# Nineteen order edges in a hybrid SSD and attention layer: small loads, state loads, attention halves, scan steps

## The chip, the cores and the metric

One core of a Trainium2 chip runs the whole program. The metric is the device time of one execution in microseconds. A run of the kernel here is three executions with their median; the profile is of one further execution. Engines are named as the profile names them: PE is TensorE, DVE is VectorE, ACT is ScalarE, POOL is GpSimd, SP is SyncE, which issues most transfers; ACT issues transfers too.

## What is computed

One layer for a prompt of 512 positions and 64 sample positions (8 sequences of 8 steps), 576 columns in all, width 1024:

```python
h = x + 0.5 * swiglu(rmsnorm(x, ffn1_norm), ...)
z, xbc, dt_raw, q, k, v, f_raw, g_ssd, g_att = split(rmsnorm(h, mix_norm) @ w_in)
xc   = silu(conv_b + sum(xa[:, j:j + L] * conv_w[j] for j in range(4)))   # xa: old rows, then xbc
y_ssd = rms_per_group((scan(xc) + d_skip * x) * silu(z)) * ssd_norm       # 4 groups, chunks of 128
y_att = fox_attention(q, k_all, v_all, logf_all)                          # 2048 cached rows for samples
h = h + (sigmoid(g_ssd) * (y_ssd @ w_ssd_proj) + sigmoid(g_att) * (y_att @ w_attn_proj)) @ w_out
y = h + 0.5 * swiglu(rmsnorm(h, ffn2_norm), ...)
```

It also returns the new keys, values, gates, SSD states and the last convolution rows.

## The kernel before

Activations lie with features on the 128 partitions and the 576 columns along the row, in two halves of 288 (`hs(0)`, `hs(1)`). Each float32 product is three matmuls of 128x288 (`mm3`, L212 to L214): high times high, low times high, high times low. A high part is a rounded copy, made by ACT; a low part is the remainder, made by DVE or, for a share of the weights, by POOL (`whi` L177, `wlo` L178; `xh` L224; `yh` L1210 and `yl` L1211 for the attention output; `ygh` L1283 and `ygl` L1284 for the gated scan output). Eight tiles of weights make 24 matmuls for a half.

The stages in order of time: the start (inputs turned on PE and scaled, small constants loaded), the first feed forward layer with the turning of the old SSD states beside it (`turns`, L365 to L389), the projections, the attention, the six convolution tiles of group 0, the attention projection, then four rounds of a group's scan with the next group's convolution tiles and output product, then the output projection and the second feed forward layer.

A convolution tile (`conv_tile`, L1135) is what most of the change hangs on. PE makes two halves into accumulators that share two banks. DVE scales the first half out of its bank (L1149) and the second in two pieces (L1154, L1156). PE turns the last columns (L1162) into the rest of the second half's bank, ACT copies that out (`tt`, L1164), and only then is that bank free. ACT starts the convolution (`kf`, L1173), DVE adds three more taps (L1175), ACT takes the tanh (L1176), and DVE makes the result in two pieces (L1177, L1179). The six tiles of a group are listed in `convs` in the order of B, C and four x tiles, so `convs[1]` is the C tile and `convs[2]` the first x tile of group 0. They write `bT`, `cT` and `xg`.

A group's scan (`group_scan`) takes the sample chunk c = 4 first, then chunks 0 to 3. A chunk makes C.B (L1307), turns x (L1330), makes its weights `dk` (L1319 to L1321) and `xdt` (L1333), multiplies (L1346, L1348) and carries the state (L1359). `state` gives the sample outputs (L1373), copied to `oo` (L1383) and turned (L1393). `gate` sums squares on POOL (L1273, L1274), `halves` makes `ygh` and `ygl`, and `group_out` begins with `rowscale`, whose matmuls L261 and L263 read these sums.

Nothing here is issued in the order of the text. A scheduler in the framework puts every engine's instructions in an order by priorities; `soon()` raises the priority, and `behind(later, first)` adds an edge that only says that `later` is put behind `first` in that order, with no wait of its own on the chip. In the kernel before all eight attention halves (`c` a copy on POOL, `h` the `yh` on ACT, and the `yl` on DVE) hang behind one tile:

```python
for x, first in zip((c, h, V.tensor_tensor(lo, y, hi.bitcast(F32), ALU.subtract)), convs[2]):
    behind(x, first)
convs.append((first, tanh, last))
```

## Time and profile before

| | us |
|---|---|
| median of 3 runs | 1869.49 (1869.19 to 1870.69) |
| the profiled execution, its own time | 1870.09 |
| its span in the trace | 1868.2 |
| PE busy | 1824.8 (98% of the span) |
| DVE busy | 1064.6 (57%) |
| ACT busy | 742.1 (40%) |
| POOL busy | 605.7 (32%) |

In the profile, times count from the start of the span. A row of the timeline gives start, duration, engine, line, operation, the tile written and the tiles read, a shape, how many such instructions follow each other, and in brackets how long the engine stood idle before it and what ended that. Engine names with a q (ACTq, SPq) are the issuing of transfers. PEclk is the clock that PE was granted, as a share of full speed. Starts of neighbouring 128x288 matmuls are some 0.13 us apart at full speed and 0.24 at half of it. The matmuls' ends are modelled and overlap.

### The profile page before, as it was taken

What the parts mean: (1) busy time and instruction counts of PE and PEld (TensorE: products, weight loads), DVE (VectorE), ACT (ScalarE), POOL (GpSimd) and SP (SyncE); (2) the same over time, 40 slices, a digit from 0 to 9 for tenths busy, and PEclk for the clock granted to TensorE, in tenths of its full rate; (3) what the DMA queues carried; (4) which work ended last, traced back from release to release, by engine and by line L of the source; (5) the groups of instructions that cost most, each with busy time, mean ns of one, the idle gap of its engine ahead of it and who ended that gap; (6) DMA issues with size and microseconds to landing.
All of it is one profiled execution on the core that took longest, in us unless ns stands there. A gap on an engine that the chain in (4) does not pass through costs nothing.

```text
span 1868.2 us, 38772 instructions
## 1 busy us (share of the span) xinstructions
PE 1824.8 (98%) x15335; PEld 1725.6 (92%) x15335; DVE 1064.6 (57%) x2309; ACT 742.1 (40%) x1555; POOL 605.7 (32%) x681
## 2 busy tenths in 40 slices
PE   7999999999999999999999999989999999999998
PEld 7999999999889888888898888878989999999998
DVE  4643334443425677876737969787695454344542
ACT  4333223334323555554426645555433333123322
POOL 0433002312322334442224644746454222002210
PEclk9999999999999999999999999999999999999999
DMA  5354443345525678885356544354472434554342
GB/s 155 121 124 127 130 138 111 119 139 164 141 80 175 190 231 244 237 227 172 91 151 185 155 125 138 103 148 139 135 216 86 124 115 131 145 144 123 109 121 67
DMA packets 297722, 269.71 MB, mean 144 GB/s; under 512 B 55068, under 2 KB 262092, under 8 KB 297388
## 3 DMA queue, kind: packets, MB, share of 16 engines
q1 hardware_dynamic: 229712, 184.16, 35.3%
q10 hardware_dynamic: 57828, 46.10, 8.0%
q0 software_dynamic: 10000, 36.97, 6.4%
q8 instruction: 121, 1.98, 0.5%
q14 instruction: 61, 0.50, 0.1%
HBM read 223.72 MB, written 38.73 MB: 140 GB/s over the span
## 4 chain that ended last, share of the span: by engine, by line
PE 63%; DVE 7%; ACT 1%; DMA 1%; issue 1%; POOL 0%; ACTq 0%; SPq 0%; DVEq 0%; POOLq 0%
PE acc L212 13%; PE acc L214 12%; PE acc L213 12%; PE pv L213 4%; PE pv L214 4%; PE pv L212 4%; PE tr L955 2%; PE tr L942 2%; PE mm L878 1%; DMA ab<-cumD 1%; PE pv L909 1%; PE mm L896 1%; DVE kf L1175 1%; PE tr L982 1%; PE pv L993 1%
## 5 line engine op out<-in xcount | busy, mean ns | idle before, releaser
L177 ACT ACTIVATE whi<-stage 128x512 fp32r<-128x512 f32 (+2 forms) x474 | 294.0, 622 | 714.8 <-PE acc L213 603.7
L212 PE MATMUL acc<-xh,whi 128*128 128x288 f32 x1792 | 541.7, 302 | 7.3 <-DVE xr L1149 4.0
L213 PE MATMUL acc<-xl,whi 128*128 128x288 f32 x1792 | 534.0, 298 | 0.0
L214 PE MATMUL acc<-xh,wlo 128*128 128x288 f32 x1792 | 532.8, 297 | 0.0
L178 DVE TENSOR_TENSOR wlo<-stage,whi 128x512 fp32r<-128x512 f32 (+1 forms) x373 | 263.7, 707 | 269.8 <-ACT whi L177 249.4
L212 PEld LDWEIGHTS acc<-xh,whi 128*128 128x128 f32 x1792 | 339.1, 189 | 14.1 <-DVE xr L1149 5.1
L213 PEld LDWEIGHTS acc<-xl,whi 128*128 128x128 f32 x1792 | 339.2, 189 | 2.9 <-issue 2.7
L214 PEld LDWEIGHTS acc<-xh,wlo 128*128 128x128 f32 x1792 | 338.8, 189 | 1.1 <-issue 0.5
L178 POOL TENSOR_TENSOR wlo<-stage,whi 128x512 fp32r<-128x512 f32 (+1 forms) x101 | 137.9, 1366 | 286.0 <-ACT whi L177 280.1
L345 POOL TENSOR_TENSOR u<-u,s 128x288 f32<-128x288 f32 x88 | 81.5, 926 | 429.0 <-DVE u L344 372.9
L212 PE MATMUL pv<-xh,whi 128*128 128x288 f32 (+1 forms) x720 | 214.1, 298 | 2.3 <-ACT xh L224 2.1
L214 PE MATMUL pv<-xh,wlo 128*128 128x288 f32 (+1 forms) x720 | 213.0, 296 | 0.0
L213 PE MATMUL pv<-xl,whi 128*128 128x288 f32 (+1 forms) x720 | 213.0, 296 | 0.0
L212 PEld LDWEIGHTS pv<-xh,whi 128*128 128x128 f32 (+1 forms) x720 | 135.0, 188 | 3.0 <-ACT xh L224 2.4
L213 PEld LDWEIGHTS pv<-xl,whi 128*128 128x128 f32 (+1 forms) x720 | 134.9, 187 | 1.2
L214 PEld LDWEIGHTS pv<-xh,wlo 128*128 128x128 f32 (+1 forms) x720 | 135.1, 188 | 0.3
L212 PE MATMUL pv<-hh,whi 128*128 128x288 f32 x352 | 106.0, 301 | 0.0
L347 POOL TENSOR_TENSOR hl<-u,hh 128x288 fp32r<-128x288 f32 x88 | 79.3, 903 | 77.5 <-ACT hh L346 77.5
L213 PE MATMUL pv<-hl,whi 128*128 128x288 f32 x352 | 104.3, 296 | 0.0
L212 PE MATMUL acc<-hh,whi 128*128 128x288 f32 x352 | 104.2, 296 | 0.0
L213 PE MATMUL acc<-hl,whi 128*128 128x288 f32 x352 | 104.2, 296 | 0.0
L214 PE MATMUL acc<-hh,wlo 128*128 128x288 f32 x352 | 104.2, 296 | 0.0
(364 smaller groups left out, 3609.8 us busy)
## 6 DMA issues: line engine op xcount, KB each, us to landing
stage<-in_w_in_dram SPq DMA_DIRECT2D x52, 512.0 KB
stage<-in_ffn_w_up_dram SPq DMA_DIRECT2D x44, 512.0 KB
stage<-in_ffn_w_gate_dram SPq DMA_DIRECT2D x43, 512.0 KB
stage<-in_ffn_w_down_dram SPq DMA_DIRECT2D x40, 512.0 KB
h<-in_state_ssm_dram SPq DMA_DIRECT2D x64, 256.0 KB
hTD<-hT ACTq DMA_DIRECT2D x32, 256.0 KB
pb<-pastD SPq DMA_DIRECT2D x32, 256.0 KB
ab<-cumD SPq DMA_DIRECT2D x32, 256.0 KB
```

The costliest lines, as they stand in the source:

```text
L177: act(hi, view, AF.Copy)
L178: e.tensor_tensor(lo, view, hi.bitcast(F32), ALU.subtract)
L212: mm(out, lhsT=hi, rhs=a, start=first and i == 0, stop=False)
L213: mm(out, lhsT=hi, rhs=b, start=False, stop=False)
L214: mm(out, lhsT=lo, rhs=a, start=False, stop=last and i == n - 1)
L345: G.tensor_tensor(u, u, sil[half], ALU.mult)
L347: G.tensor_tensor(hl[:, hs(half)], u, hh[:, hs(half)].bitcast(F32), ALU.subtract)
L878: mm(s[:, :n], lhsT=q, rhs=ks[2 * self.p + e][:, :n], start=hl == 0, stop=hl == 1)
L896: nc.tensor.transpose(t[:, j * P:(j + 1) * P], lt[:, j * P:(j + 1) * P], ident)
L909: mm(self.ob[o:o + 32, i * P:(i + 1) * P], lhsT=vtok[j][:, v0:v0 + 32], rhs=self.pts[e][:, j * P:(j + 1) * P], start=j == 0, stop=j == i)
L942: nc.tensor.transpose(t[:, i * P:(i + 1) * P], kk[:, i, p * P:(p + 1) * P], ident)
L955: mm(s[kv * 32:(kv + 1) * 32, :], lhsT=self.q(kv), rhs=self.kT[kv // 2], start=True, stop=True)
```

## The change

It adds edges, moves three loads to another queue, and changes no arithmetic. In the diff `ev` is L1156, `turned` L1162, `cb` L1307, `x` L1330 and then L1393, `own` L1346, `m1` and `m2` are L261 and L263, and `lows` are the `ygl`.

- A. Three small loads on ACT (`bb` twice, `al`; L497, L498, L502) go behind the eighth `xh` of the start.
- B. The first three loads of old states (L379) are issued by ACT instead of SP.
- C. The eight attention halves (copy, `yh`, `yl`) go behind `convs[1]` to `convs[4]`, two each, instead of all behind `convs[2]`.
- D. The last two `ygl` of the first half (`lows[2:4]`) go behind L1156 of the next group's B tile.
- E. C.B and three of the x turns of the sample chunk go behind the turned columns (L1162) of the group's own x tiles.
- F. Three of the four turns of `oo` (L1393) go behind the first product of a later chunk.
- G. The matmuls of `rowscale` in groups 0 to 2 go behind L1162 of the next group's C tile.

```diff
-            q.dma_start(out=bb[:32], in_=A["dt_bias"].rearrange("o h -> h o"))
-            q.dma_start(out=bb[32:48], in_=A["b_f"].rearrange("o h -> h o"))
+            behind(q.dma_start(out=bb[:32], in_=A["dt_bias"].rearrange("o h -> h o")), nrm1.insts[7])
+            behind(q.dma_start(out=bb[32:48], in_=A["b_f"].rearrange("o h -> h o")), nrm1.insts[7])
...
-            q.dma_start(out=al[:32], in_=A["a_log"].rearrange("o h -> h o"))
+            behind(q.dma_start(out=al[:32], in_=A["a_log"].rearrange("o h -> h o")), nrm1.insts[7])
...
-                        nc.sync.dma_start(out=tiles[n], in_=ap3(A["state_ssm"][0], *place(n % 2, n // 2)))
+                        (nc.scalar if n < 3 else nc.sync).dma_start(out=tiles[n], in_=ap3(A["state_ssm"][0], *place(n % 2, n // 2)))
...
-        convs.append((first, tanh, last))
+        convs.append((first, tanh, last, ev, turned))
...
-                for x, first in zip((c, h, V.tensor_tensor(lo, y, hi.bitcast(F32), ALU.subtract)), convs[2]):
+                for x, first in zip((c, h, V.tensor_tensor(lo, y, hi.bitcast(F32), ALU.subtract)), convs[1 + n // 2]):
                     behind(x, first)
...
+                if c == 4:
+                    behind(cb, convs[6 * g + 2][4])
...
+                    if c == 4 and i < 3:
+                        behind(x, convs[6 * g + 3 + i][4])
...
+                    if r == 0:
+                        owns.append(own)
...
+                if i < 3:
+                    behind(x, owns[i + 2])
...
+            if first is not None:
+                behind(m1, first)
+                behind(m2, first)
...
-            rg = rowscale(ysq, 1.0 / 512, ysq)
+            rg = rowscale(ysq, 1.0 / 512, ysq, convs[6 * g + 7][4] if g < 3 else None)
...
+                for x in lows[2:4]:
+                    behind(x, convs[6 * g + 6][3])
```

What it makes of the order is seen at three places. Lines of the changed kernel are higher by 2 at L261, by 5 around L1149 to L1211, by 7 at L1330.

**DVE, convolution tiles of group 0.** The accumulators `acc_2231` and `acc_2232` are the halves of the third x tile, `xr_2210`, `xr_2219` and `xr_2230` the first three x tiles. Before:

```order
L1211 TENSOR_TENSOR yl_2245_12103<-qy_1293_7508,yh_2244_12102 128x576
L1211 TENSOR_TENSOR yl_2247_12108<-qy_1420_8071,yh_2246_12107 128x576
L1211 TENSOR_TENSOR yl_2249_12113<-qy_1547_8637,yh_2248_12112 128x576
L1211 TENSOR_TENSOR yl_2251_12118<-qy_1674_9203,yh_2250_12117 128x576
L1211 TENSOR_TENSOR yl_2253_12123<-qy_1801_9769,yh_2252_12122 128x576
L1149 TENSOR_TENSOR xr_2230_11948<-acc_2231_11951,rbc_901_5369 128x288
L1211 TENSOR_TENSOR yl_2255_12128<-qy_1928_10335,yh_2254_12127 128x576
L1211 TENSOR_TENSOR yl_2257_12133<-qy_2055_10901,yh_2256_12132 128x576
L1211 TENSOR_TENSOR yl_2259_12138<-qy_2156_11390,yh_2258_12137 128x576
L1175 SCALAR_TENSOR_TENSOR kf_2223_11928<-xr_2219_11865,P2_80_293,kf_2223_11928 128x600 x2
L178 TENSOR_TENSOR wlo_2264_12150<-stage_2261_12143,whi_2263_12149 128x512
L1175 SCALAR_TENSOR_TENSOR kf_2223_11928<-xr_2219_11865,P2_80_293,kf_2223_11928 128x600
```

Now, from the end of the first x tile:

```order
L1184 SCALAR_TENSOR_TENSOR xg_2203_11773<-xr_2210_11786,kf_2214_11849 128x64
L1216 TENSOR_TENSOR yl_2249_12113<-qy_1547_8637,yh_2248_12112 128x576
L1216 TENSOR_TENSOR yl_2251_12118<-qy_1674_9203,yh_2250_12117 128x576
L1180 SCALAR_TENSOR_TENSOR kf_2223_11928<-xr_2219_11865,P2_80_293,kf_2223_11928 128x600
L1154 TENSOR_TENSOR xr_2230_11948<-acc_2231_11951,rbc_901_5369 128x288
L1180 SCALAR_TENSOR_TENSOR kf_2223_11928<-xr_2219_11865,P2_80_293,kf_2223_11928 128x600 x2
L178 TENSOR_TENSOR wlo_2264_12150<-stage_2261_12143,whi_2263_12149 128x512
L1159 TENSOR_TENSOR xr_2230_11948<-acc_2232_11977,rbc_901_5369 128x224
L1161 TENSOR_TENSOR xr_2230_11948<-acc_2232_11977,rbc_901_5369 128x8x8
L1182 SCALAR_TENSOR_TENSOR xg_2203_11773<-xr_2219_11865,kf_2223_11928 128x512
L1184 SCALAR_TENSOR_TENSOR xg_2203_11773<-xr_2219_11865,kf_2223_11928 128x64
L1216 TENSOR_TENSOR yl_2253_12123<-qy_1801_9769,yh_2252_12122 128x576
```

Of the six `yl` between the first x tile and the third tap of the second, two are left there. One pair now stands behind the C tile, ahead of these rows, and two pairs behind later tiles. The L1149 of the third x tile (now L1154) stands behind two `yl` and one tap where it stood behind five `yl`.

**PE, the same place.** Here the rows carry what they wait for: a semaphore of DVE or of ACT. Before:

```order
L214 MATMUL acc_2231_11951<-xh_898_5358,wlo_2229_11945 128x288
L1162 MATMUL acc_2221_11894<-ident_2_76,xr_2219_11865 91x128 [waits DVE_49]
L1330 MATMUL mm_2351_12741<-ident_2_76,xg_2203_11773 64x128 [waits DVE_49]
L212 MATMUL acc_2232_11977<-xh_793_4687,whi_2226_11940 128x288 [waits DVE_49]
L213 MATMUL acc_2232_11977<-xl_794_4688,whi_2226_11940 128x288
...
L214 MATMUL acc_2232_11977<-xh_898_5358,wlo_2229_11945 128x288
L212 MATMUL acc_2240_12030<-xh_793_4687,whi_2235_12019 128x288 [waits Activation_49]
L213 MATMUL acc_2240_12030<-xl_794_4688,whi_2235_12019 128x288
```

Now:

```order
L214 MATMUL acc_2231_11951<-xh_898_5358,wlo_2229_11945 128x288
L1167 MATMUL acc_2221_11894<-ident_2_76,xr_2219_11865 91x128 [waits DVE_49]
L1337 MATMUL mm_2351_12741<-ident_2_76,xg_2203_11773 64x128 [waits DVE_49]
L212 MATMUL acc_2232_11977<-xh_793_4687,whi_2226_11940 128x288 [waits Activation_49]
L213 MATMUL acc_2232_11977<-xl_794_4688,whi_2226_11940 128x288
...
L214 MATMUL acc_2232_11977<-xh_898_5358,wlo_2229_11945 128x288
L212 MATMUL acc_2240_12030<-xh_793_4687,whi_2235_12019 128x288 [waits DVE_49]
L213 MATMUL acc_2240_12030<-xl_794_4688,whi_2235_12019 128x288
```

PE's order is the same. The second half of the third x tile waited for DVE, for the L1149 of its own first half; now it waits for ACT, for the copy `tt` of the tile before it. The half behind it has the two the other way round: the two banks are handed out in another turn.

**PE, the start of group 2's output product.** `acc_2955` and `acc_2956` are the halves of one of the next group's convolution tiles. Before:

```order
L1162 MATMUL acc_2944_15982<-ident_2_76,xr_2942_15953 91x128 [waits DVE_49]
L214 MATMUL acc_2955_16040<-xh_898_5358,wlo_2953_16034 128x288
L261 MATMUL tr_2988_16349<-ssq_2815_15409,cst_1_75 128x512 [waits PE_49,Pool_49]
L212 MATMUL acc_2956_16066<-xh_793_4687,whi_2950_16029 128x288 [waits DVE_49]
L213 MATMUL acc_2956_16066<-xl_794_4688,whi_2950_16029 128x288
L214 MATMUL acc_2956_16066<-xh_793_4687,wlo_2951_16030 128x288
```

Now:

```order
L1167 MATMUL acc_2944_15982<-ident_2_76,xr_2942_15953 91x128 [waits DVE_49]
L214 MATMUL acc_2955_16040<-xh_898_5358,wlo_2953_16034 128x288
L212 MATMUL acc_2956_16066<-xh_793_4687,whi_2950_16029 128x288 [waits DVE_49]
L213 MATMUL acc_2956_16066<-xl_794_4688,whi_2950_16029 128x288
L214 MATMUL acc_2956_16066<-xh_793_4687,wlo_2951_16030 128x288
L212 MATMUL acc_2956_16066<-xh_807_4780,whi_2950_16029 128x288
L263 MATMUL tr_2988_16349<-ssq_2815_15409,cst_1_75 128x512 [waits PE_49,Pool_49]
L213 MATMUL acc_2956_16066<-xl_808_4781,whi_2950_16029 128x288
```

The matmul that reads the sums of squares (L261, now L263) stands four matmuls later, and the first of these four is one that waits for DVE.

## Rows read from the trace of the kernel before

**Rows 1.** The page's first part: busy time, share of the span, instructions.

```profile
PE 1824.8 (98%) x15335; PEld 1725.6 (92%) x15335; DVE 1064.6 (57%) x2309; ACT 742.1 (40%) x1555; POOL 605.7 (32%) x681
```

**Rows 2.** Waits of PE: engine line, waited for, total us, times, longest us.

```profile
PE tr L261 <- POOL ssq L1274: 3.2, 1, 3.2
...
PE pv L212 <- ACT xh L224: 2.1, 1, 2.1
PE tr L1393 <- ACT oo L1383: 2.1, 1, 2.1
```

**Rows 3.** Stretches: length, busy PE, PEld, DVE, ACT, POOL, then PEclk, DMA.

```profile
911.95:918.90 6.95, 6.85 (x52) 6.54 (x52) 5.76 (x9) 3.18 (x6) 2.39 (x3) 1.00 0.02 4
933.30:936.80 3.50, 3.50 (x17) 3.50 (x17) 2.49 (x5) 0.78 (x2) 0.41 (x1) 0.54 0.01 3
...
1240.30:1243.70 3.40, 3.40 (x16) 3.39 (x15) 3.13 (x6) 0.51 (x1) 0.95 (x2) 0.50 0.82 260
```

**Rows 4.** Timeline of ACT and its issues at the start.

```profile
13.78 0.78 ACT L224 ACTIVATE xh<-h,P 128x576 fp32r<-128x576 f32 x1 [1.75 <-DMA stage<-in_ffn_w_gate_dram]
...
14.28 0.40 ACTq L502 DMA_DIRECT2D al<-in_a_log_dram  x1
...
34.04 4.87 ACTq L508 DMA_DIRECT2D pcol<-in_page_table_dram  x7
```

**Rows 5.** Waits of SP's queue, 110 to 125 us.

```profile
SPq L379 <- DMA pastD<-lg: 2.6, 2, 1.9
```

**Rows 6.** Timeline of SP's queue, 117 to 122 us.

```profile
120.85 1.47 SPq L379 DMA_DIRECT2D h<-in_state_ssm_dram  x3
```

**Rows 7.** Timeline of PE at the first turned state.

```profile
123.90 0.90 PE L385 MATMUL tr<-ident,h 128*128 128x128 f32 x4 [2.65 <-DMA h<-in_state_ssm_dram]
```

**Rows 8.** Timeline of PE in the convolution tiles of group 0.

```profile
924.11 0.40 PE L212 MATMUL acc<-xh,whi 128*128 128x288 f32 x1 [1.70 <-DVE xr L1149]
...
931.74 0.35 PE L1162 MATMUL acc<-ident,xr 128*91 128x128 f32 x1 [1.01 <-DVE xr L1156]
932.91 0.30 PE L1330 MATMUL mm<-ident,xg 128*64 128x128 f32 x1 [0.82 <-DVE xg L1179]
```

**Rows 9.** Timeline of DVE there.

```profile
920.25 3.44 DVE L1211 TENSOR_TENSOR yl<-qy,yh 128x576 fp32r<-128x576 f32 x5
923.61 0.45 DVE L1149 TENSOR_TENSOR xr<-acc,rbc 128x288 f32<-128x288 f32 x1
923.98 3.18 DVE L1211 TENSOR_TENSOR yl<-qy,yh 128x576 fp32r<-128x576 f32 x3
...
928.71 1.78 DVE L178 TENSOR_TENSOR wlo<-stage,whi 128x512 fp32r<-128x512 f32 x1
```

**Rows 10.** Timeline of ACT there.

```profile
918.65 4.69 ACT L1210 ACTIVATE yh<-qy 128x576 fp32r<-128x576 f32 x8
...
924.55 0.25 ACT L1164 ACTIVATE tt<-acc 91x128 f32<-91x128 f32 x1
```

**Rows 11.** Timeline of POOL there.

```profile
923.94 1.94 POOL L178 TENSOR_TENSOR wlo<-stage,whi 128x512 fp32r<-128x512 f32 x1 [2.86 <-ACT whi L177]
928.25 1.70 POOL L178 TENSOR_TENSOR wlo<-stage,whi 128x512 fp32r<-128x512 f32 x1 [2.37 <-ACT whi L177]
```

**Rows 12.** Line L1211: count, duration least, median and most in ns.

```profile
L1211 DVE TENSOR_TENSOR yl<-qy,yh x8: 744/746/1850, 920.3 to 926.4; 128x576 fp32r<-128x576 f32 x8
```

**Rows 13.** Timeline of DVE in the scan of group 1.

```profile
1129.04 3.54 DVE L1284 SCALAR_TENSOR_TENSOR ygl<-xg,P,ygh 128x288 fp32r<-128x288 f32 x4
1132.50 0.45 DVE L1149 TENSOR_TENSOR xr<-acc,rbc 128x288 f32<-128x288 f32 x1
```

**Rows 14.** Timeline of PE in the scan of group 2.

```profile
1224.32 0.45 PE L1346 MATMUL pv<-dk,xdt 128*64 128x128 f32 x4
```

**Rows 15.** Timeline of ACT there.

```profile
1220.02 1.28 ACT L1319 ACTIVATE dk<-ab,TT 128x128 f32<-128x128 f32 x4 [7.15 <-DMA ab<-cumD]
```

**Rows 16.** Timeline of DVE ahead of group 2's output product.

```profile
1238.90 0.45 DVE L1149 TENSOR_TENSOR xr<-acc,rbc 128x288 f32<-128x288 f32 x1
```

More of the change, by code (lines that the diff above doesn't have):

```diff
@@ L214, in mm3, with hilo @@
             mm(out, lhsT=lo, rhs=a, start=False, stop=last and i == n - 1)
-    def hilo(hp, view, tagh, tagl, scale=None, n=NT, bufs=None):
+    def hilo(hp, view, tagh, tagl, scale=None, n=NT, bufs=None, insts=None):
         hi = tl(hp, [P, n], F32R, tag=tagh, bufs=bufs)
@@ L223, in hilo @@
         else:
-            act(hi, view, AF.Copy, scale=scale)
+            h = act(hi, view, AF.Copy, scale=scale)
             V.scalar_tensor_tensor(lo, view, scale, hi.bitcast(F32), ALU.mult, ALU.subtract)
+            if insts is not None:
+                insts.append(h)
         return hi, lo
@@ L255, in spread, with rowscale @@
         return r
-    def rowscale(s, inv, r):
+    def rowscale(s, inv, r, first=None):
         with soon():
             t = tr()
-            mm(t, lhsT=C("one"), rhs=s[:, :NP], start=True, stop=True)
+            m1 = mm(t, lhsT=C("one"), rhs=s[:, :NP], start=True, stop=True)
             t2 = sm()
-            mm(t2[:, :NS], lhsT=C("one"), rhs=s[:, NP:], start=True, stop=True)
+            m2 = mm(t2[:, :NS], lhsT=C("one"), rhs=s[:, NP:], start=True, stop=True)
+            if first is not None:
+                behind(m1, first)
+                behind(m2, first)
             V.transpose(r[:, :NP], t)
@@ L275, in __init__ @@
         def __init__(self, wcol, sqp=None, xsp=xp):
-            self.wcol, self.xs, self.n, self.sqp, self.xsp = wcol, [], 0, sqp, xsp
+            self.wcol, self.xs, self.n, self.sqp, self.xsp, self.insts = wcol, [], 0, sqp, xsp, []
         def add(self, h, squares=True):
             k = self.n
-            self.xs.append(hilo(self.xsp, h, "xh", "xl", scale=P1[:, self.wcol + k:self.wcol + k + 1]))
+            self.xs.append(hilo(self.xsp, h, "xh", "xl", scale=P1[:, self.wcol + k:self.wcol + k + 1], insts=self.insts))
             self.n += 1
@@ L1155, in conv_tile @@
         with soon():
-            V.tensor_tensor(xsamp[:, :, 3:], a[:, NP - HT:].rearrange("p (b t) -> p b t", t=T),
+            ev = V.tensor_tensor(xsamp[:, :, 3:], a[:, NP - HT:].rearrange("p (b t) -> p b t", t=T),
                             rbc[:, NP:].rearrange("p (b t) -> p b t", t=T), ALU.mult)
@@ L1161, in conv_tile @@
             t = full[:n, 512 - P:]
-            nc.tensor.transpose(t, xr[:, NP:], ident)
+            turned = nc.tensor.transpose(t, xr[:, NP:], ident)
             tt = tl(xz, [n, P], tag="tt", bufs=1)
@@ L1262, in group_scan @@
             ysq = tl(sa, [P, NT], tag="ssq", bufs=2)
-            yhl = []
+            yhl, lows, owns = [], [], []
             def gate(o0, n):
@@ L1283, in halves @@
                     act(hi, xg[:, i, hs(half)], AF.Copy, scale=w)
-                    V.scalar_tensor_tensor(lo, xg[:, i, hs(half)], w, hi.bitcast(F32), ALU.mult, ALU.subtract)
+                    lows.append(V.scalar_tensor_tensor(lo, xg[:, i, hs(half)], w, hi.bitcast(F32), ALU.mult, ALU.subtract))
             def operands(x, bp):
@@ L1306, in chunk @@
                 s = sm()
-                mm(s[:n, :n], lhsT=bT[:, o0:o0 + n], rhs=cT[:, o0:o0 + n], start=True, stop=True)
+                cb = mm(s[:n, :n], lhsT=bT[:, o0:o0 + n], rhs=cT[:, o0:o0 + n], start=True, stop=True)
+                if c == 4:
+                    behind(cb, convs[6 * g + 2][4])
                 cbm = tl(wk, [P, P], tag="cbm", bufs=3)
@@ L1329, in chunk @@
                 for i in range(4):
-                    nc.tensor.transpose(t[:n, i * P:(i + 1) * P], xg[:, i, o0:o0 + n], ident)
+                    x = nc.tensor.transpose(t[:n, i * P:(i + 1) * P], xg[:, i, o0:o0 + n], ident)
+                    if c == 4 and i < 3:
+                        behind(x, convs[6 * g + 3 + i][4])
                 xdt = tl(wk, [P, 8, 64], tag="xdt", bufs=2)
@@ L1345, in chunk @@
                     ov = yb[(r % 2) * 64:(r % 2 + 1) * 64, (r // 2) * n:(r // 2 + 1) * n]
-                    mm(ov, lhsT=xdt[:n, r, :], rhs=dks[r // 4][:n, r % 4, :n], start=True, stop=not 0 < c < 4)
+                    own = mm(ov, lhsT=xdt[:n, r, :], rhs=dks[r // 4][:n, r % 4, :n], start=True, stop=not 0 < c < 4)
+                    if r == 0:
+                        owns.append(own)
                     if 0 < c < 4:
@@ L1392, in group_scan @@
             for i in range(4):
-                nc.tensor.transpose(t[:, i * P:(i + 1) * P], oo[:, i * P:(i + 1) * P], ident)
+                x = nc.tensor.transpose(t[:, i * P:(i + 1) * P], oo[:, i * P:(i + 1) * P], ident)
+                if i < 3:
+                    behind(x, owns[i + 2])
             for i in range(4):
@@ L1408, in group_scan @@
                                 in_=oo.rearrange("p (i n) -> p i n", n=P))
-            return ysq, yhl
+            return ysq, yhl, lows
         def group_out(g, ysq, ys_):
-            rg = rowscale(ysq, 1.0 / 512, ysq)
+            rg = rowscale(ysq, 1.0 / 512, ysq, convs[6 * g + 7][4] if g < 3 else None)
             cw = Cols(A["w_ssd_proj"][0], 0, k0=4 * g, nk=4)
@@ L1440, in build @@
             cur = nxt
-            gated = group_scan(g, *cur)
+            *gated, lows = group_scan(g, *cur)
             if g < 3:
                 nxt = group_in(g + 1)
+                for x in lows[2:4]:
+                    behind(x, convs[6 * g + 6][3])
             for _ in range((3, 0, 0, 5)[g]):
```

## The prediction

> **What bounds the kernel now.** PE is busy for 1824.8 of 1868.2 us [rows 1], so only the 43 us in which it stands idle can be won, and the slow stretches that follow some of them. I read three views in this order. First the waits of PE, to see which idle times the edges touch [rows 2]. Then the timeline of PE around each. A stall costs more than its idle time where the clock falls behind it: after the pair of 1.01 and 0.82 us [rows 8] and after the 3.17 us ahead of L261 PE was granted 0.54 and 0.50 of full speed for 3.5 and 3.4 us [rows 3], that is the 1.2 GHz level, worth 1.7 us each. The single stall of 1.70 us [rows 8] was not followed by one. Last the timelines of the engines that PE waited for. A difference under 0.2% (3.74 us) I call the same.
>
> **The sum, part by part.** The work is the same; every gain is a stall that goes.
>
> A, the three small loads. ACT was ready 1.75 us before its first `xh` [rows 4]; the wait stood on a small load's issue ahead of it, for a weight tile that `xh` doesn't read. Now `xh` is next on ACT and the wait falls on the weight's high part behind it. PE waited 2.13 us for that `xh` [rows 2]. At most PE is 1.8 us earlier. The bound from below is 0.95: PE's next work needs the second half of the inputs, for which the issue at 14.28 had waited too [rows 4]; they may have landed only then, 0.95 us before PE came to them. I take **1.2**. The loads now stand ahead of the eight page table loads, 0.65 to 0.7 us of ACT's queue each [rows 4]. The page indices and the weights behind them on ACT come up to 2 us later; PE first needs what hangs on them about 1.6 us after they would then be ready. If that cover is gone, each us beyond it is lost.
>
> B, three state loads on ACT. SP was free and its issue stood until 120.85 [rows 6], for stores of `pastD` [rows 5]. The issue on ACT waits for the same stores. It loses the queue's own delay and its longer first issue: three issues took 1.47 us, and the transfer that PE waited for until 123.90 [rows 7] landed 3.05 us after the first. I take **0.4**. From below it is -0.3, if the issues on ACT stand behind a late tanh; from above 1.2, if the stores' landing is not what held it. Behind them on ACT a high part and the first layer's own steps come 1 to 2 us later; PE needs that high part 8 us on. The stall keeps over 2 us, so its slow stretch stays too. The Trainium skill (DMA: Bandwidth & Descriptors, "Issuing engines are not separate DMA queues") says that issuing from several engines saves only the sequencer's time, since all land on the same 16 DMA engines. By that sentence this part is worth nothing and the sum 0.4 less; no run here has shown it yet.
>
> C, the attention halves, is the main term. In the kernel before ACT made all eight `yh` in one piece [rows 10] and `tt` came behind them at 924.55, so the bank of the second x tile was held; the third tile's second half was given the bank of its own first half instead, and waited for L1149, which stood on DVE behind five `yl` of 3.44 us [rows 9]. That is the 1.70 us stall. Three more `yl` and a slow `wlo` then made the next tile's L1156 and L1179 late: 1.01 and 0.82 us, with the slow stretch of 1.7 [rows 3, 8, 9]. Together 3.53 + 1.7 = 5.2 us. In the new order ACT has two `yh` at a time (1.2 us), so `tt` of each tile follows its L1162 by 0.3 us, and DVE has two `yl` per tile. Following the new order with the durations of the rows, the third tile's second half starts at 922.45 instead of 924.11, and the fourth's at 929.5 instead of 932.98, both after a wait of 0.35 for `tt`. L1149 has 3 us to spare, since the half that now waits for it comes a half later. The last pair of `yl` is read by the attention projection's own first product, some 2.4 us after it starts, and is ready at about that time: up to 0.5 there. I take 5.2 less 0.7 = **4.5**; bounds 2.5, with 2 us of waiting for the last pair, and 5.2.
>
> D, `ygl` behind L1156. In group 1 the four `ygl` (3.54 us) stand behind that L1156 already and still ahead of the L1149 for which PE waits until 1133.00 [rows 13]. They keep that place. Elsewhere a DVE step changes places with one of 0.4 to 0.9 us, in the first group's scan ahead of an `xdt` that PE reads. I take **-0.3**, bounds -1.5 and 1.8, the whole stall.
>
> E, C.B and the x turns. In the group where PE waits for C.B, it stood behind that L1162 already. **0**, bounds -0.3 and 1.1.
>
> F, the turns of `oo`. PE waits 2.11 us for `oo` in group 2 [rows 2]. The third turn now stands behind the next product, and PE runs on for 2.7 us of matmuls. But the next product, L1346, reads `dk`, and ACT stood idle 7.15 us until 1220.02 for its load [rows 15]; `dk` and `xdt` let L1346 begin at 1224.32 [rows 14], by ACT's and DVE's order, which is the same. PE comes there 2 us earlier and waits there. **0**, bounds -0.3 and 2.1.
>
> G, the sums of squares. L261 waited 3.17 us for POOL [rows 2] until 1239.34. The first of the four matmuls that now stand ahead of it reuses a bank that L1149 empties, and DVE came to that L1149 at 1238.90 and was done with it at 1239.35 [rows 16], behind a tap that waited for ACT. So PE still stops and goes on at the same time, and the slow stretch stays. **0**, bounds -0.3 and 4.9.
>
> Sum: 1.2 + 0.4 + 4.5 - 0.3 = 5.8. From the profiled 1870.09 that makes 1864.3; the median of the runs is 0.6 lower, so 1863.7.
>
> **The rivals.**
>
> R1: the scan edges do what they are for. Then the 2.11 and 3.17 us go, with 1.7 of slow clock [rows 2, 3]: 7.0 more, 1856.7. For it: PE has work of its own at both places. Against it: the next wait ends at the same time [rows 14, 16].
>
> R2: only the first stall of the tiles goes, since the rest of the tile's work on DVE is as late as before. A at its low end and 1.70 of C, less 0.3: 2.4, 1867.1. For it: DVE is busy 5.76 of 6.95 us in a tile without any `yl` [rows 3], and a pair adds 1.25 to 1.4 [rows 9, 12], so it is full.
>
> R3, slower: DVE becomes the bound of four tiles. Some of its steps take 1.1 us longer while POOL makes a `wlo`: one `yl` took 1850 against 744 ns, a `wlo` 1.78 [rows 9, 11, 12]. The 5.76 holds one such step; with a pair and two more a tile takes DVE 5.76 + 1.3 + 2.2 = 9.25 against PE's 6.95. Over four tiles 9.2 us, less the 3 that L1149 has to spare, is 6.2; three stalls of 2 us each followed by a slow stretch add 5.1; the 5.2 of before go, and 1.3 of A, B and D: 4.8 slower than before, 1874.3. It decides from about two more slow steps a tile. Against it: POOL makes one `wlo` in a tile, which can hold up one step of DVE. The Trainium skill (SBUF — State Buffer, "SBUF: two separate sides") says that a DVE instruction with two SBUF inputs and a GpSimd one that reads SBUF lock each other out for the whole instruction. The 1850 ns agree, and by that rule the change puts more such instructions of DVE beside POOL's.
>
> **How the numbers follow.** The forecast as summed 0.65, R1 0.10, R2 0.17, R3 0.08. The forecast's own range, from C at 2.5 with A at 0.95 and B at 0 to C at 5.2 with A at 1.8, B at 1.2, is 1866.3 to 1861.6. Of its 0.65 some 0.02 end within 3.74 of the old time. Faster: 0.63 + 0.10 = 0.73. Same: 0.17 + 0.02 = 0.19. Slower 0.08. The range for 8 in 10 takes in R1 and R2 with 1.5 us for the bounds of D: 1856.5 to 1868.5; R3 is left out.
>
> **What would show it.** Right: PE's first `pv` L212 near 13 us; no wait for L1149 over 0.5 us between 915 and 935 and full clock there, with `yl` in four pairs; PE still waiting for state loads, for a product in group 2's scan at its old time, and for a DVE step ahead of L261. Wrong: full clock after group 2's scan (R1), a stall in the tiles at another line (R2), or DVE without a gap from 905 to 935 and PE waiting in each tile (R3).

## The result and the profile after

The changed kernel took 1873.13 us (median of 20 runs, 1868.84 to 1879.58), the kernel before beside it 1869.36 us (20 runs): ratio 1.0023, 95% interval 1.0016 to 1.0031. By the ratio it is slower by 4.3 us (the two medians differ by 3.8); I had forecast 5.8 us faster, in a range that ends at 1868.5. The profiled execution is the slowest of the 20 (1879.58 us), so its own total says little; what follows is read place by place.

The page's first part, which answers [rows 1]:

```profile
PE 1833.4 (98%) x15335; PEld 1730.1 (92%) x15335; DVE 1061.0 (57%) x2309; ACT 742.8 (40%) x1555; POOL 602.9 (32%) x681
```

The instructions are the same in number, yet PE is busy for 8.6 us more. It stood in slow stretches for longer: between the start and the last stage it was granted half the clock for 30.6 us (from 122.8, 583.6, 1051.2, 1160.4 and 1249.2 us on), in the kernel before for 13.6 (from 124.1, 584.9, 933.1 and 1240.3). Half of that difference is 8.5 us. The waits of PE, with columns as in [rows 2]:

```profile
PE pv L1355 <- DVE xdt L1342: 5.2, 4, 2.4
PE acc L212 <- DVE xr L1154: 4.5, 3, 3.2
...
PE tr L390 <- DMA h<-in_state_ssm_dram: 4.2, 1, 4.2
...
PE mm L1312 <- DVE cT L1184: 2.0, 1, 2.0
```

The waits of [rows 2] for `ssq` and `oo` are gone, and that for `xh` is down to 0.25 us. These four have grown: in the kernel before they were 1.2 us for `xdt`, 4.0 for `xr`, 2.6 for the state load and 1.1 for `cT`. The timeline of PE gives their places (the brackets hold the idle time and what ended it):

```profile
123.90 1.09 PE L390 MATMUL tr<-ident,h 128*128 128x128 f32 x4 [4.22 <-DMA h<-in_state_ssm_dram]
...
927.13 0.40 PE L212 MATMUL acc<-xh,whi 128*128 128x288 f32 x1 [0.25 <-ACT tt L1169]
...
946.66 0.40 PE L212 MATMUL acc<-yh,whi 128*128 128x288 f32 x1 [1.48 <-DVE sq L1240]
...
1049.81 0.45 PE L1355 MATMUL pv<-dk,xdt 128*64 128x128 f32 x4 [2.36 <-DVE xdt L1342]
...
1158.73 0.33 PE L1312 MATMUL mm<-cT,bT 128*64 128x64 f32 x2 [2.04 <-DVE cT L1184]
...
1248.38 0.40 PE L212 MATMUL acc<-xh,whi 128*128 128x288 f32 x1 [3.16 <-DVE xr L1154]
```

Five readings. At the first states PE waits 4.22 us, where it waited 2.65 [rows 7]. In the four convolution tiles the stalls of 1.70, 1.01 and 0.82 us [rows 8] are gone; two of 0.25, for `tt`, are left. A stall of 1.48 us is new just behind the tiles, one of 2.36 in the scan of group 0. At 1158 PE waits 2.04 us for `cT`, ahead of C.B. And at 1248 PE waits as long as it had waited for `ssq`, now for L1154. Four stretches (columns as in [rows 3]):

```profile
119.60:124.00 4.40, 0.18 (x2) 0.13 (x2) 2.96 (x5) 2.48 (x6) 2.00 (x3) 0.86 0.90 245
...
126.00:129.40 3.40, 3.40 (x16) 3.40 (x16) 0.46 (x1) 0.00 (x0) 0.80 (x1) 0.50 0.46 154
...
583.60:593.80 10.20, 10.20 (x39) 8.70 (x39) 9.74 (x26) 3.64 (x8) 2.76 (x5) 0.50 0.60 155
...
1051.00:1058.00 7.00, 6.77 (x39) 3.96 (x40) 6.76 (x14) 4.22 (x14) 2.33 (x6) 0.52 0.44 118
```

Behind the stalls of 4.22 and 2.36 us PE was granted half the full speed (the 1.2 GHz level). At 583.6 us it was granted no more, and there is no stall: PE had work without a gap, small matmuls that read 24 partitions.

```profile
580.77 1.98 PE L702 MATMUL tr<-hr,bias 24*128 24x512 f32 x4
...
582.98 3.06 PE L815 MATMUL mm<-hr,vv 24*128 24x64 f32 x16
```

To place gains and losses I compare the start of the same matmul by its number in the two traces ("offset", after less before; behind 1040 us F's order gives some numbers to other matmuls): -1.6 us at 18 us, +1.0 at 129, +4.3 at 614, +4.6 at 920, +2.0 at 947, +1.6 at 1040, +6.8 at 1054, +9.8 at 1168, +7.3 at 1223, +9.1 at the end. The 3.3 us lost between 129 and 614 come in and behind the slow stretch at 587, which no edit touches; the last section comes back to it.

### The profile page after: what moved, and what is told of

The parts are those of the page before. It is cut to its first block, busy times and chain, and to the rows that moved or that the text cites. A ratio compares the mean times of both kernels' runs of the same rounds, so it can differ in the third digit from the quotient of the medians.

```text
span 1877.7 us, 38792 instructions
## 1 busy us (share of the span) xinstructions
PE 1833.4 (98%) x15335; PEld 1730.1 (92%) x15335; DVE 1061.0 (57%) x2309; ACT 742.8 (40%) x1555; POOL 602.9 (32%) x681
## 4 chain that ended last, share of the span: by engine, by line
PE 65%; DVE 5%; DMA 2%; ACT 1%; issue 1%; POOL 0%; ACTq 0%; SPq 0%; DVEq 0%
PE acc L212 13%; PE acc L214 13%; PE acc L213 13%; PE pv L213 4%; PE pv L214 4%; PE pv L212 4%; PE tr L960 2%; PE tr L947 2%; PE mm L883 1%; DMA ab<-cumD 1%; PE pv L914 1%; PE mm L901 1%; PE pv L1355 1%; DVE kf L1180 1%; PE tr L987 1%; PE pv L998 1%
## 5 line engine op out<-in xcount | busy, mean ns | idle before, releaser
L212 PE MATMUL acc<-xh,whi 128*128 128x288 f32 x1792 | 542.0, 302 | 7.3 <-DVE xr L1154 4.5
L212 PEld LDWEIGHTS acc<-xh,whi 128*128 128x128 f32 x1792 | 339.7, 190 | 14.2 <-DVE xr L1154 6.4
L212 PE MATMUL pv<-xh,whi 128*128 128x288 f32 (+1 forms) x720 | 214.0, 298 | 0.2 <-ACT xh L224 0.2
L212 PEld LDWEIGHTS pv<-xh,whi 128*128 128x128 f32 (+1 forms) x720 | 134.9, 187 | 0.9 <-ACT xh L224 0.5
L212 PE MATMUL pv<-hh,whi 128*128 128x288 f32 x352 | 105.9, 301 | 0.0
L212 PE MATMUL acc<-hh,whi 128*128 128x288 f32 x352 | 104.1, 296 | 0.0
```

The source lines that it names most:

```text
L212: mm(out, lhsT=hi, rhs=a, start=first and i == 0, stop=False)
```

## The experiments

Each ratio below is to the kernel before, run beside it on the same chip, with its 95% interval; chips differ by up to 6 us, so times are not compared across chips. Part letters are the prediction's.

**The parts alone.** Four kernels with one part of the diff each; D to G went together.

> Only the three small loads are moved (A). The prediction's theory: 1.2 us faster than before (0.95 to 1.8), PE's first product of the first layer near 13 us, the rest of the trace as before and merely earlier. Rival: the start is earlier by 1.5 us but the wait for the old states, 2.65 us at 123.9 before, takes it back because their landing does not move with PE; then that wait is above 4 us and the time is within 0.5 us of before. Told apart by the start of the first matmul after the state load and by the length of that wait.

> Only the first three state loads are issued by ACT (B). The prediction's theory: 0.4 us faster (-0.3 to 1.2), the wait for the first state load 2.2 us. Rival, from the trace of the whole change, where that wait grew to 4.22 us while the fourth state load went out on SP at 118.65, just before the three on ACT at 118.75: the fourth load is no longer behind the first three and shares the transfer engines with them, so the first lands 5 us after its issue and not 3; the wait is 3 to 4.5 us, the stretch at half clock behind it longer, and the time 0.5 to 2.5 us more than before.

> Only the attention halves are spread over four tiles (C). The prediction's theory: 4.5 us faster (2.5 to 5.2), no wait over 0.5 us in the convolution tiles nor behind them. Rival, from the trace of the whole change: the stalls of 1.70, 1.01 and 0.82 us and the stretch at half clock go, but the last pair of low halves and the taps put with them make DVE late for the attention projection's first results, with a wait of 1.5 us at L1235 and one of 0.4 us at a low half; then 2.5 to 3.3 us faster.

> Only the edges of the scans (D to G). The prediction's theory: within 0.5 us of before, the waits of group 2 at their old places. Rival, from the trace of the whole change, where PE's lead over before shrank by some 5.5 us between 1042 and 1058 and by 2.7 us between 1140 and 1165 and grew by 0.5 later: these edges cost 4 to 8 us, with a wait of 2 us or more for xdt in the scan of group 0 followed by a stretch at half clock. If that wait is absent here and the time is as before, it belonged to that one execution or to the change's other parts, which shift when transfers land.

| kernel | ratio | interval |
|---|---|---|
| A | 0.9999 | 0.9988 to 1.0010 |
| B | 1.0019 | 1.0009 to 1.0029 |
| C | 0.9988 | 0.9976 to 1.0000 |
| D to G | 1.0018 | 1.0008 to 1.0027 |

The four differences add up to +0.0024, the whole change has +0.0023: it loses by B and by the scan's edges, and C gains less than these cost. b_alone, c_alone and scan_alone went the way of their rivals, scan_alone with 3.4 us by its ratio where its rival had 4 to 8. a_alone's time can't tell its two theories apart; its wait for the states was 2.88 us, not the over 4 of its rival. The order of instructions shows one thing more: D, E or G by itself leaves every engine's order as it was. The order of D to G together is that of F alone, which moves steps on all engines and in all four groups. The later place of `rowscale`'s matmul in group 2, which the prediction puts down to G, comes with F.

**B: which load is late.** On SP alone the first load was issued at 120.85 [rows 6] and PE had its tile 3.05 us later [rows 7]. After the change (the queues of SP and ACT in the timeline):

```profile
118.65 6.73 SPq L384 DMA_DIRECT2D h<-in_state_ssm_dram  x2
...
118.75 1.53 ACTq L384 DMA_DIRECT2D h<-in_state_ssm_dram  x3
```

ACT issues 2.1 us earlier, and PE starts at the same 123.90: landing took 5.15 us. SP, rid of three loads, issues the fourth at the same moment. The earlier issue is not the queue's doing, since the stores ahead of it went out earlier too. The last of them before, then after, in the timeline of ACT:

```profile
116.27 0.39 ACTq L562 DMA_DIRECT2D pastD<-lg  x1
...
114.75 0.38 ACTq L567 DMA_DIRECT2D pastD<-lg  x1
```

From the last store's issue to the first load's it took 3.8 to 4.6 us in the eleven executions with the loads on SP and 3.9 to 4.4 in the eight with them on ACT, on average 4.1 in both.

This kernel puts the fourth on ACT too, behind the three:

```diff
-                        (nc.scalar if n < 3 else nc.sync).dma_start(out=tiles[n], ...
+                        (nc.scalar if n < 4 else nc.sync).dma_start(out=tiles[n], ...
```

> As B alone, but the first four state loads go out on ACT instead of three, so none goes out on SP beside them. Theory 1: with three on ACT the fourth, free to start on SP at 118.7, shares the transfer engines with the first, which then lands 5.2 to 5.8 us after its issue instead of 3 to 3.9; here the first is alone at the head of one queue and lands 3 to 4 us after 118.8, PE's wait for it is 1 to 2.5 us, and the time is within 1 us of before or up to 1.5 us less. Theory 2: ACT's queue is itself slower, behind the 32 stores of small pieces that it carries just before; then the wait stays at 3.5 us or more and the time 2 to 4 us above before, as with three.

Ratio 1.0002 (0.9991 to 1.0013). Its timeline of ACT's queue and of PE:

```profile
120.69 1.52 ACTq L384 DMA_DIRECT2D h<-in_state_ssm_dram  x3
122.45 0.37 ACTq L384 DMA_DIRECT2D h<-in_state_ssm_dram  x1
...
123.73 0.63 PE L390 MATMUL tr<-ident,h 128*128 128x128 f32 x4 [1.85 <-DMA h<-in_state_ssm_dram]
```

Landing 3.04 us, wait 1.85. Over all profiled executions, from the first issue to PE's start: 3.1 to 4.5 us in eleven with all loads on SP, 5.1 to 5.8 in three with three on ACT and the fourth on SP, 3.0 to 4.4 in five with four on ACT. PE's mean wait is 2.4, 4.2 and 2.4 us. The fourth load goes out 0.1 us ahead of the first in the three, and 1.5 to 1.8 us behind it in the other sixteen. So the fourth load beside the other three is what B costs. The slow stretch behind this wait went with its length: none in the eight executions with waits of 1.57 to 2.16 us, 3.4 us in the nine with 2.17 to 3.64, 6.8 us in the two with 4.22 and 4.82.

**C: the new stall behind the tiles.** DVE's timeline after the change, at the step that PE waits for at 946.66:

```profile
946.15 0.45 DVE L1240 SCALAR_TENSOR_TENSOR sq<-kf,acc 128x288 f32<-128x288 f32 x1 [1.94 <-DMA kf<-thD]
```

The first `th` of the attention projection takes a buffer that the taps of the tiles use (tag "kf"); it was issued at 940.41, when a tap had freed it. With a buffer of its own:

```diff
-                th = tl(mixp, [P, NT], tag="kf", bufs=2)
+                th = tl(mixp, [P, NT], tag="kf", bufs=2) if j else tl(yhp, [P, NT], tag="thl", bufs=1)
```

> As C alone, but the first load for the gate of the attention projection gets a buffer of its own and can be issued early; with C alone it shares the buffer of a convolution's taps, was issued at 933.5 and landed near 938.4, and DVE waited 1.15 us for it and PE 0.70 for DVE. Theory 1: this load is what takes back a part of C; then PE's wait at L1235 (0.70 with C alone, 1.48 with the whole change) is gone, and the time is 0.7 to 1.5 us below C alone. Theory 2: DVE is simply late after the tiles, with low halves and taps ahead; then PE's wait stays at 0.5 us or more.

Ratio 0.9984 (0.9973 to 0.9995), against 0.9988 for C: the interval now leaves 1 out. The two intervals overlap, so what the buffer is worth is read from the traces. DVE's `sq` and PE's first product there:

```profile
944.00 0.45 DVE L1240 SCALAR_TENSOR_TENSOR sq<-thl,acc 128x288 f32<-128x288 f32 x1 [0.34 <-PE acc L214]
...
940.52 0.40 PE L213 MATMUL acc<-yl,whi 128*128 128x288 f32 x1 [0.37 <-DVE yl L1216]
```

DVE now waits for PE there. PE's wait for `sq` is 0.70, 1.48 and 1.63 us in the three executions with C as it is, and gone in the five with the buffer. From 920 to 947 us the offset falls by 2.5 to 3.4 us in the three executions with C as it is and by 4.2 in all five with the buffer; in the eleven without C it moves by 0 to -1.8, on average by -0.7.

**F: where the scan's edges cost.** F's edges in group 0 only, then in group 1 only:

```diff
-                if i < 3:
+                if i < 3 and g == 0:
                     behind(x, owns[i + 2])
```

> Of the edges in the scans only the turns of the sample outputs of group 0 (F in group 0). Theory 1: F alone moves work in the scans (D, E and G leave every place as it was), and in group 0 it turns PE's short wait at those turns (0 to 2.3 us at 1041) into one of 2 us or more at the next product, where xdt stands on DVE behind four low halves that wait for ACT, with a stretch at half clock behind it: 2 to 4 us between 1040 and 1054 and 1.5 to 3.5 us in the time. Theory 2: the loss between 1040 and 1054 comes from the load of the decay rows landing late, which varies by execution; then this run loses no more there than the kernels without F (0 to 2.4 us) and its time is that of before.

> Only the turns of group 1 (F in group 1). Theory 1: the wait of 1.8 us for L1149 at 1133 goes, and in its place come waits of 1.1 us at the next tile and 1.6 to 2.0 us at C.B, with a stretch at half clock: 0.6 us won by 1138, 2.5 to 3 us lost between 1140 and 1168, 1.5 to 2.5 us slower in all. Theory 2: those waits need the delay that the edges make in group 0; then they are absent here and the time is that of before.

1.0014 (1.0004 to 1.0024) and 1.0014 (1.0001 to 1.0026). In f_g0 PE waits 2.40 us for `xdt` at 1051, as at 1049.81 above. The chain behind that wait, in the timelines of SP, ACT and DVE after the change:

```profile
1038.23 0.76 SPq L1321 DMA_DIRECT2D ab<-cumD  x1
...
1044.74 0.40 ACT L1326 ACTIVATE dk<-ab,TT 128x128 f32<-128x128 f32 x1 [5.33 <-DMA ab<-cumD]
...
1047.06 2.09 DVE L1289 SCALAR_TENSOR_TENSOR ygl<-xg,P,ygh 128x288 fp32r<-128x288 f32 x4 [2.83 <-ACT ygh L1288]
1049.08 0.68 DVE L1342 TENSOR_TENSOR xdt<-mm,TT 128x512 f32<-128x512 f32 x1
```

`xdt` stands behind four `ygl`, these wait for `ygh`, and those stand on ACT behind a `dk` that waits for its load, 6.5 us after the issue. Either the order of `ygh` and `ygl` or the load could be mended. The first:

```diff
+            for u, l in zip(ups, lows):
+                behind(u, last3["exp"])
+                behind(l, last3["xdt"])
```

(`ups` and `lows` are the `ygh` and `ygl` steps, `last3` the second `dk` Exp and the `xdt` of chunk 3.)

> Part F alone (whose order of instructions is that of D to G together, 1.0018 of the kernel before), and besides, in every group, the four early ygh of the scan put behind the second dk Exp of chunk 3 on ACT, and the four early ygl behind xdt of chunk 3 on DVE. Theory queue: F costs time because the ygl that it brings ahead of xdt wait for ygh, and these for a dk that waits for its cumD load; then the xdt wait of 2.0 to 2.4 us at about 1048 falls under 0.5 us, the local offset of 1040 to 1054 falls from +3.2..5.2 to about +1, and the ratio from 1.0018 to about 1.0005. Rival load: the late cumD load itself holds TensorE, whatever stands in the queues; then a wait of about 2 us stays there, on dk instead of xdt, and the ratio stays at 1.0014 to 1.0020. Rival elsewhere: F's cost is mostly in group 1 (f_g1 alone 1.0014); then the xdt wait goes and the ratio stays above 1.0010.

Ratio 0.9996 (0.9985 to 1.0007), and no wait there is over 0.50 us. But the load landed in 4.2 us here, so this run can't tell the two theories apart. The next three turn to the load: F's new order of SP's loads in the kernel before, by one edge on SP (`scan_order_sp`), F with the two weight loads behind that load (`scan_load_first`), and the same two loads moved in the kernel before (`load_first`).

```diff
+            if g == 1:
+                behind(staged[n0 + 10], scts[2])
```

```diff
+            if g == 0:
+                for x in staged[n0 + 10:n0 + 12]:
+                    behind(x, cums[9])
```

(`staged`, `scts` and `cums` list the `stage`, `scT` and `ab` loads; the first edit is `scan_order_sp`'s.)

> The kernel before, with none of the change's edges, and on SP alone at group 0 the order that part F brings: the second scT load ahead of the first stage load, so that the cumD load of chunk 3's second half (ab) is issued right behind that stage load (some 0.5 us after it, where it was 1.0). Theory load: F's cost in group 0 is this load's landing; then it lands 6.1 to 6.5 us after its issue (3.97 in the profile of before), TensorE waits 2.0 to 2.4 us at about 1047, and the ratio is 1.0010 to 1.0018. Theory queue: the order of ygh and ygl costs it; then the landing takes 4 to 5 us, the wait is under 0.8 us and the ratio 0.9992 to 1.0006. Third: the landing varies from one execution to the next whatever the order; then it may be anything from 4.0 to 6.5 us, and the ratio is within 0.0006 of 1.

> Part F alone (its order is that of D to G together), and in group 0 the two stage loads behind the cumD load of chunk 3's second half on SP. Theory load: it then lands 4 us or less after its issue and earlier, the wait for xdt at about 1047 goes (under 0.4 us), and the ratio falls from 1.0018 to 1.0003 to 1.0010 (group 1 keeps its own part). Theory queue: ygl still stand ahead of xdt, behind ygh behind dk; if dk's load lands late for another reason the wait stays at 1.5 to 2.4 us, and the ratio at 1.0012 to 1.0020.

> The kernel before, with none of the change's edges; only the two stage loads of group 0 behind the cumD load of chunk 3's second half on SP. Waits of 0 to 2.4 us (mean 1.2 in seven profiled executions without F in group 0) stand at about 1047 in such kernels. Theory load: they are gone here, landing 4 us or less, ratio 0.9990 to 0.9998. Rival: the weights come later by as much and TensorE waits for wlo or whi instead: ratio 1.0000 to 1.0008.

| kernel | ratio | interval | issue to `dk`, us |
|---|---|---|---|
| scan_order_sp | 1.0000 | 0.9989 to 1.0012 | 4.4 |
| scan_load_first | 0.9990 | 0.9979 to 1.0002 | 3.9 |
| load_first | 1.0008 | 0.9998 to 1.0019 | 4.4 |

Over all 19 profiled executions PE's wait at that place goes with the load's landing, whichever step it is put down to: up to 4.8 us from issue to `dk` no wait is over 0.8 us but one of 1.08, at 5.4 and 5.7 us it is 1.4 and 1.7, from 6.1 us on 2.0 to 2.4. Where it is put down to `oo`, in seven executions without F in group 0, the wait is the landing less 4.0 us; where it is put down to `xdt`, in the four with F as it stands, it is the landing less 4.1. So at a late landing F's order costs no more than the order before. But F as it stands landed in 6.1 to 6.5 us in four executions of four, F with either repair in 3.7 to 4.2 in three of three, and kernels without F in group 0 took 4.0 to 4.8 in eight of twelve and 5.4 to 6.4 in four. One of those four is f_g1, whose wait can't come from its own edges, which begin later:

```profile
1051.32 0.48 PE L1400 MATMUL tr<-ident,oo 128*128 128x128 f32 x1 [2.36 <-ACT oo L1390]
```

So F costs by this load, as far as four late landings in four against four in twelve show it, and with either repair the cost is gone; scan_load_first came out below its range of 1.0003 to 1.0010. F's order of SP's loads did not bring the cost (scan_order_sp falls to the rival), but that run is no clean test: in its trace the one edge has moved steps on every engine, 36 on DVE, and `xdt` stands ahead of a `ygl` there. Moving the load in the kernel before gains nothing (load_first falls to its rival). In the four executions of F as it stands the weight load ahead of it had stood waiting too and was issued 1.4 us after `scT`, directly ahead of `ab`; in scan_order_sp 0.5 us after it. Which of these neighbours makes it late is not settled.

f_g1's ratio is not explained either. In its profiled execution the offset stands at 11.1 us at 1058 and at 9.3 at the end, so its edges in group 1 cost nothing there, and one late load in one execution doesn't make a median of twelve.

**The parts put together.** `best` is A, C, B with four loads on ACT, and the buffer of c_own; `best_halves` adds the edges of f_halves without F, `best_load` those of load_first. `after_again` is the changed kernel once more. `mended` is the whole change, A to G, with the three repairs (four loads on ACT, own buffer, load first).

> Parts A and C, B with all four first state loads on ACT, and a buffer of its own for the first th of the attention halves; D to G left off. If the parts add up as they did for the change as a whole, -1.2 us at the start, 0 to -1 at the state loads and -3 at the four convolution tiles: ratio 0.9972 to 0.9984. If A and C interact (a part ends in slack of the other), 0.9984 to 0.9995. The waits at 924 to 947 stay under 0.5 us each; the one at 124 is 1.5 to 2.2 us.

> The kernel best, with the early ygh and ygl of every group behind chunk 3's second dk Exp and xdt, without F. Theory queue: three of the four ygl stand ahead of xdt in the kernel before too, and the xdt waits of 0 to 2.4 us at about 1048 come from there; then they are gone here and the time is 0 to 2 us below best (ratio to before 0.9965 to 0.9980). Rival load: no change against best, within 0.0008.

> The kernel best (A, C, B with four loads on ACT, own buffer for the first th), and the two stage loads of group 0 behind the cumD load. Theory load: 0 to 1.5 us below best, ratio to before 0.9966 to 0.9976. Rival: no difference from best, 0.9974 within its interval of 0.0012.

> The changed kernel once more. What belongs to its order of instructions returns: the wait of 3.5 to 4.3 us for the first state load, waits of 1.5 to 2.5 us for xdt at 1050, 1.0 to 1.5 for the convolution's accumulator or sq at 947, 2.0 for C.B at 1159, 3.2 for xr at 1248. What belongs to one execution does not: half-clock stretches of 24 matmuls at 588 and 20 at 125 need not return, and their numbers may be anything from 7 to 24. Ratio 1.0016 to 1.0031 again.

> The whole change, A to G, with three repairs: the fourth state load on ACT behind the other three, a buffer of its own for the first th, and group 0's two stage loads behind the cumD load of chunk 3's second half. Theory: the change loses by B's fourth load, by th's buffer and by that cumD load, and by nothing else; then the waits at about 122 (under 2.9 us), 947 (none) and 1050 (under 0.8 us) are mended, and the ratio is that of best and of scan_load_first together, 0.9960 to 0.9978. Rival: the order of D to G also costs something in groups 1 and 2 (C.B 2.0 us at 1159, xr 3.2 us at 1248); then A, B and C gain their 0.2 to 0.26% and the scan gives some of it back: 0.9980 to 0.9995. If neither holds, 1.0000 or more.

| kernel | ratio | interval |
|---|---|---|
| best | 0.9974 | 0.9962 to 0.9987 |
| best_halves | 0.9979 | 0.9968 to 0.9990 |
| best_load | 0.9984 | 0.9972 to 0.9995 |
| after_again | 1.0013 | 0.9999 to 1.0027 |
| mended | 0.9977 | 0.9965 to 0.9988 |

The repairs turn 1.0013 to 1.0023 into 0.9977, within the theory's range, though the interval reaches into the rival's (0.9980 to 0.9995). So the three steps are the change's loss as far as these runs can tell, and what the scan's edges cost in groups 1 and 2, if anything, is within the interval. In `mended` the three places read, in the timeline of PE, and the load on SP and ACT:

```profile
122.86 0.63 PE L391 MATMUL tr<-ident,h 128*128 128x128 f32 x4 [2.06 <-DMA h<-in_state_ssm_dram]
...
939.45 0.40 PE L214 MATMUL acc<-yl,whi 128*128 128x288 f32 x1 [0.37 <-DVE yl L1217]
...
1044.39 0.45 PE L1356 MATMUL pv<-dk,xdt 128*64 128x128 f32 x4 [0.62 <-DVE xdt L1343]
...
1033.45 0.41 SPq L1322 DMA_DIRECT2D ab<-cumD  x1
...
1037.15 0.40 ACT L1327 ACTIVATE dk<-ab,TT 128x128 f32<-128x128 f32 x1 [3.48 <-DMA ab<-cumD]
```

`best` needs none of D to G and is as fast; neither edge added to it gains; best_load misses the 0.9966 to 0.9976 of its theory. `best` and `mended` both beat the kernel before and the changed one, by 4.9 and 4.3 us against the former, by their ratios. after_again brought back the waits of the order (4.82 us for the state load, 2.05 for `xdt`, 1.63 for `sq`, 3.17 for L1154), but 1.37 for C.B where 2.0 was expected. It has a slow stretch of 6.8 us at 125 again, but only 6.8 at 586 where the first profile had 10.2. Its ratio is below the 1.0016 that was expected at least.

## Why the prediction was wrong, by its own steps

The signs that I had named for being right all came: `pv` L212 at 12.63 us, no wait for L1149 in the tiles and full clock there, `yl` in four pairs, waits for state loads, for group 2's next product and for a DVE step ahead of L261. One of them looks at a place where time was lost, the state loads, but it asks for a wait and not for its length; none looks at `th` or at group 0's scan.

**A** (1.2, bounds 0.95 to 1.8): right at its place, and smaller behind it. PE's matmul at 14.61 starts 1.2 to 2.3 us earlier in the seven executions with A (mean 1.8) and 0.5 earlier on average in those without: 1.3, of which 0.8 is left at 18 us, below my lower bound. It is too small for the run times to show.

**B** (+0.4): wrong sign, and the failed step is "It loses the queue's own delay and its longer first issue". There was no such delay to lose: between the last store and the first load lie 4.1 us on either queue, and the first issue took 0.37 us on SP and 0.41 on ACT. And I followed the three loads that moved and not the fourth that stayed. It had been issued behind them; freed of them it starts with them and the landing grows from 3.05 to 5.15 us, past my lower bound of -0.3. The slow stretch behind grows as well where the wait passes 4 us. From 117 to 129 us the three kernels with three loads on ACT lose 0.7 to 3.7 us, mean 2.4; the eleven with all loads on SP gain 1.0 on average, the five with four on ACT 0.9. The 3.4 between the first two is near B's 0.19%, which is 3.5 us, though b_alone's own profile is the 0.7. The Trainium skill (DMA: Bandwidth & Descriptors, "Issuing engines are not separate DMA queues"), which I quoted against any gain, says that loads of different engines interleave on the same 16 DMA engines. The landing times agree; taken further, that sentence warns of just this loss.

**C** (4.5): the mechanism was right. All three stalls go, `tt` leaves 0.25 to 0.36, and the last pair of `yl` costs 0.37 where I allowed 0.5. The size was off twice. The step "Together 3.53 + 1.7" took the slow stretch behind the tiles as certain; it stands there in five of eleven executions without C, behind stalls that are the same to 0.03 us in ten of them. And "the attention projection's own first product" was followed for `yl` only, not for `th`, whose load waits for a tap's buffer: 0.70 to 1.63 us. By the offsets of 920 and 947 us, with the 0.7 of the executions without C taken off, C is worth 2.1 us as it is (mean 2.8) and 3.5 with the buffer.

**D, E, G** (-0.3, 0, 0): right that they bring nothing. They move nothing, and D's forecast change of places doesn't come about. What I foresaw for G comes with F: the wait for `ssq` became one of 3.16 us for L1154, as said with [rows 16].

**F** (0): right in group 2, where I looked. PE runs on and waits at the next product, for `xdt`, where it had waited 2.11 us for `oo`:

```profile
1233.29 0.45 PE L1355 MATMUL pv<-dk,xdt 128*64 128x128 f32 x4 [1.93 <-DVE xdt L1342]
```

The failed step is that "the third turn now stands behind the next product" was costed at the one stall that it was meant for. The same edge acts in every group and turns the scheduler's order on all engines, and in group 0 it made a load late that ACT, DVE and PE wait for in turn: 0.14 to 0.18%. Where PE waits for `oo` there without F, it waits for `xdt` with it, and at the same landing no longer; the landing is what grew.

**R3**, the slower rival, had the sign and not the cause. The eight `yl` took 745 to 766 ns and none was slowed, but taps behind them were, as here beside a `wlo` on POOL:

```profile
926.06 1.85 DVE L1180 SCALAR_TENSOR_TENSOR kf<-xr,P,kf 128x600 f32<-128x600 f32 x1
...
925.48 1.79 POOL L178 TENSOR_TENSOR wlo<-stage,whi 128x512 fp32r<-128x512 f32 x1
```

Other taps took 0.84 us. The Trainium skill's rule on the shared port (SBUF — State Buffer, "SBUF: two separate sides") agrees with these rows; a tile holds about one such step, as "Against it" says, DVE kept its share of 57% [rows 1], and PE waits no more than 0.25 us at a time in these tiles. R1 didn't come, and R2's 1867.1 neither.

## What to carry to other kernels

When loads move to another queue, follow those that stay: whatever stood behind the moved ones now starts beside them, and the tile that is read first lands later. Put the whole run of loads on one queue in the order of their use. An ordering edge is costed in every place where its line runs and for all that the scheduler turns around it, not at the stall that it was made for. And when a stall goes, look at the next step's operands one by one, the loads that wait for a buffer too. A sign of being right is wanted for each place that an edit can reach, not only for those where a gain is expected.

## What the runs showed of the hardware

The first of three state loads landed in 3.0 to 4.5 us with the fourth issued 1.5 to 1.8 us behind it, and in 5.1 to 5.8 with the fourth issued 0.1 us ahead of it. Between the first issue and the landing the DMA share was 0.72 in the first profile of before and 0.74 in b_four, against 0.92 in that of the changed kernel and 0.85 in b_alone.

PE's clock fell to the 1.2 GHz level in two ways here. Behind the wait for the state loads it went with the wait's length, as told under B. At about 587 us, where no edit acts, it fell in all 19 executions without a wait: within a run of 26 small matmuls that read 24 partitions, or up to 0.6 us behind it, and PE had no gap there. There the slow stretch was 3.4 us long in twelve executions, 6.8 in two and 10.2 in five. Behind the three stalls of the tiles it came in five executions of eleven. At half the speed 3.4 us are worth 1.7, so a slow stretch in one profile need not be a property of the kernel; I had put it into the sum as one.

The stretch from 614 to 900 us takes longer on some chips, with or without the change. Its offset grows by 4.1 to 6.1 us in nine executions on three chips (best, mended, b_four and after_again among them), and by -1.4 to 2.1 in eight on two others and in the first profile of the changed kernel. The kernel before took 1873.5 to 1873.9 us on the three, 1867.8 and 1868.0 on the two.
